# The first norm's weight row broadcast by TensorE into PSUM, its loads and the first weight loads issued together, one square pass per token tile

## The chip, the cores and the metric

One NeuronCore of a Trainium2 chip runs the whole program. The metric is device time in microseconds of one execution, the median of three runs. Five engines work beside each other: TensorE (PE) multiplies, VectorE (DVE), ScalarE (ACT) and GpSimd (POOL) do elementwise work, and SyncE (SP) issues most of the DMA transfers. Each takes its own instructions strictly in the order in which the program was scheduled, and waits where an operand is not ready.

## The reference: one hybrid decoder layer

The layer has 512 tokens of width 1024. Three residual blocks follow one another, each with an RMS norm before and after it: a token mixer (sparse attention, pooling and a spatial gating unit, all fed by one projection `w_in`), cross-attention into 256 memory tokens, and a gated MLP with a causal convolution. Everything is float32. The change touches only the very start:

```python
def rms_norm(x, g):
    xf = x.astype(F32)
    y = xf * lax.rsqrt(jnp.mean(xf * xf, axis=-1, keepdims=True) + EPS)
    return (y * g.astype(F32)).astype(x.dtype)
...
        h = rms_norm(x, mix_norm_pre[l])
        proj = h @ w_in[l]
        q, kc, vc, ksl, vsl, kw, vw, gt, pin, u, v = jnp.split(proj, IN_SPLITS, axis=-1)
```

## The kernel before

**The numbers.** A float32 matmul is made of three: both operands are split into a rounded high part and a low remainder (`split`: ACT casts the high part, another engine subtracts for the low part), and `mm3` (lines 167 to 169) adds high x high, high x low and low x high in PSUM. So each 1024-column piece of weights passes through a raw tile (`wr`), a cast into `wh` and a subtraction into `wl` before TensorE may use it, and each normed activation goes into `hTh` and `hTl`.

**The first norm.** Tokens are cut into four tiles of 128 rows (`xt[0]` to `xt[3]`). For each, `norm_T` squares the row on ACT in two halves of 512 columns (L108, the sums go through `ss` into `nt` on DVE), takes the power -0.5 on POOL (L100, `nr`), multiplies by that scale and the norm's weight row on DVE (L119, `hn`), transposes 128x128 blocks on TensorE (L122, into `tp`, two PSUM buffers), and splits the result into `hTh` (ACT, L67) and `hTl` (DVE, L68). The tile `hn` has two buffers, so a third `hn` waits for the transposes of the first. The weight row `grow` (1x1024) is needed on all 128 partitions: L252 lets POOL copy it there into `gpre`.

**The first projections.** `w_c` holds the 256 columns of `w_in` for the compressed branch, `w_k` those for the keys. `chan_halves` runs four jobs (two 128-column blocks of each) first over tokens 0 to 255 (half 0: tiles 0 and 1), then over tokens 256 to 511: 2 x 4 x 8 x 3 = 192 matmuls of 256 columns. Then come the fp32 matmuls of the compression (L367), the query projection of group 0 (`w_q`), and the value projection (columns 280 wide, four quarter loads of `w_in` through `wr`), and then attention.

**What sets the order.** The tile scheduler arranges each engine's instructions by a timeline of its own; after that each engine is in order. SP issues the loads in one row, so a load that has to wait for a buffer holds back the loads behind it. Raw weight tiles `wr` have three buffers. The pool `xp` (the start's tiles) is freed after the first norm, and its memory is used by tiles of the next stages, whose first writer waits for the old tile's last reader. POOL issues its own DMAs too: `fscr` and `cb` (L303 to L309), the tables of position biases that go through DRAM.

Of the kernel before, what the change touches and what calls it, by code (L numbers as in the profile page):

```python
# [49 lines left out]
def trunk_kernel(ctx, tc, x, mem, rel_bias, mix_norm_pre, mix_norm_post, w_in, cmp_pos, cmp_w1,  # L50
# [49 lines left out]
        nc.gpsimd.tensor_tensor(r, t, neghalf[:, :n], OP.pow)  # L100
        return r

    def norm_T(src, g, dst, i, junk, hn, pstile):
        t = None
        for half in range(2):
            ss = small("ss")[:, 0:1]
            c = slice(half * 512, half * 512 + 512)
            nc.scalar.activation(junk, src[:, c], AF.Square, accum_out=ss)  # L108
            t2 = small("nt")[:, 0:1]
            if half == 0:  # L110
                nc.vector.tensor_scalar(t2, ss, 1.0 / D, EPS, OP.mult, OP.add)
            else:
                nc.vector.scalar_tensor_tensor(t2, ss, 1.0 / D, t, OP.mult, OP.add)
            t = t2
        r = power(t, 1)
        for half in range(2):
            h = hn(half)
            c = slice(half * 512, half * 512 + 512)
            nc.vector.scalar_tensor_tensor(h, src[:, c], r, g[:, c], OP.mult, OP.mult)  # L119
            pt = pstile()  # L120
            for k in range(4):
                tr = nc.tensor.transpose(pt[:, k, :], h[:, k * P:(k + 1) * P], ident)  # L122
            o = (slice(None), i // 2, slice(half * 4, half * 4 + 4), slice(i % 2 * P, i % 2 * P + P))
            done = split(dst[0][o], dst[1][o], pt)
        return (tr,) + done
# [19 lines left out]
            if done is not None:  # L145
                done(c)

    def wload(parts, nk, ncol, pool=None, engs=(None, None)):
        pool = pool or wpool
        hi = pool.tile([P, 2048], F32R, name="wh")  # L150
        lo = pool.tile([P, 2048], F32R, name="wl")
        n = nk // 2 * ncol
        for half in range(2):
            raw = wpool.tile([P, 1024], F32, name="wr", bufs=3)
            rv = raw[:, :n].rearrange("p (k c) -> p k c", k=nk // 2)
            c0 = 0
            for src in parts:
                w = src.shape[1]
                sr = src.rearrange("(k p) c -> p k c", p=P)
                nc.sync.dma_start(rv[:, :, c0:c0 + w], sr[:, half * nk // 2:(half + 1) * nk // 2, :])  # L160
                c0 += w
            split(hi[:, half * n:half * n + n], lo[:, half * n:half * n + n], raw[:, :n], engs[half])
        return (hi[:, :2 * n].rearrange("p (k c) -> p k c", k=nk),
                lo[:, :2 * n].rearrange("p (k c) -> p k c", k=nk))
# [52 lines left out]
    with ExitStack() as at:  # L217
# [26 lines left out]
        with ExitStack() as p0:  # L244
            xp = pool_of(p0, "xp")
            xt = [xp.tile([P, D], F32, name=f"xt{i}") for i in range(TT)]
            grow = xp.tile([1, D], F32, name="grow")
            gpre = xp.tile([P, D], F32, name="gpre")
            nc.sync.dma_start(xt[0], x[0:P, :])
            nc.sync.dma_start(grow, mix_norm_pre)  # L250
            nc.sync.dma_start(xt[1], x[P:2 * P, :])
            nc.gpsimd.partition_broadcast(gpre, grow)  # L252
            idi = xp.tile([P, P], mybir.dt.int32, name="idi")
            nc.gpsimd.iota(idi, pattern=[[1, P]], base=0, channel_multiplier=-1)
            nc.vector.tensor_scalar(ident, idi, 0.0, None, op0=OP.is_equal)
            junk = xp.tile([P, 512], BF16, name="junk")

            def norm0(i):
                norm_T(xt[i], gpre, hT, i, junk,
                       lambda k: xp.tile([P, 512], F32, name="hn", tag="hn", bufs=2), tp_tile)  # L260

            norm0(0)
            norm0(1)
            w_c = wload([w_in[:, 512:768]], KT, 256, engs=(nc.gpsimd, nc.gpsimd))
            for i in range(2, TT):
                nc.sync.dma_start(xt[i], x[i * P:(i + 1) * P, :])
            w_k = wload([w_in[:, 768:896], w_in[:, 1024:1152]], KT, 256,
                        engs=(nc.gpsimd, (nc.vector, nc.gpsimd)))
            for i in range(2, TT):
                norm0(i)  # L270

            smA = xp.tile([P, P], F32, name="smA")
            smB = xp.tile([89, P], F32, name="smB")
# [675 lines left out]
```

## Time and profile before

| what | us |
|---|---|
| median of 3 runs | 801.93 |
| lowest and highest run | 801.47, 803.82 |
| profiled execution, first to last instruction | 802.6 |
| TensorE busy in it | 757.6 (94%) |
| VectorE, ScalarE, GpSimd busy | 452.7, 352.9, 128.1 |

The profiled execution gives its span only; no time around the span is shown. The span lies 0.7 us above the median and inside the spread of the three runs. "Busy" is the time an engine spends in instructions; for TensorE the ends of matmuls are modelled, so that 94% says that it seldom waits, and nothing about its peak.

### The profile page before, as it was taken

The page shows a single profiled execution, that of the slowest core. Times are in us where ns is not written, and L with a number is a line of the kernel's source. Part 1 is how long each engine was busy: PE and PEld are TensorE (multiplying, and loading weights), DVE is VectorE, ACT ScalarE, POOL GpSimd, SP SyncE. Part 2 cuts the span into 40 slices and gives each one's busy share as a digit, 9 for nine tenths or more (in the row PEclk, how much of TensorE's full clock was granted, in tenths as well). Part 3 has the DMA queues.
Part 4 walks back from the last instruction along what each step waited for, and adds up shares of the span by engine and source line. Part 5 has one row for each costly group of instructions (what it writes and reads, how often), then busy time and mean ns, then how long its engine had stood idle before and what let it go on. Part 6 is the DMA issues. An engine that isn't in the chain of part 4 may idle for free.

```text
span 802.6 us, 10783 instructions
## 1 busy us (share of the span) xinstructions
PE 757.6 (94%) x4164; PEld 655.8 (82%) x4164; DVE 452.7 (56%) x796; ACT 352.9 (44%) x645; POOL 128.1 (16%) x144
## 2 busy tenths in 40 slices
PE   0699999998999999999999999999999999999996
PEld 0598988876998889988888988888888888888884
DVE  0864557899666584328366475665655665213214
ACT  2334558667655463336354443444343344113111
POOL 1633246476510110040002000000000000000001
PEclk9999999999999999999999999999999999999998
DMA  5455314401048136320150123333233333124212
GB/s 197 109 132 142 115 30 131 158 23 31 3 147 318 58 114 202 106 77 30 53 183 28 53 79 106 105 105 94 80 90 105 105 105 105 56 76 146 75 42 105
DMA packets 65163, 80.64 MB, mean 100 GB/s; under 512 B 4079, under 2 KB 48071, under 8 KB 65112
## 3 DMA queue, kind: packets, MB, share of 16 engines
q1 hardware_dynamic: 64791, 79.77, 31.6%
q8 instruction: 33, 0.54, 0.3%
q0 software_dynamic: 320, 0.18, 0.1%
q14 instruction: 19, 0.15, 0.1%
HBM read 77.79 MB, written 2.14 MB: 100 GB/s over the span
## 4 chain that ended last, share of the span: by engine, by line
PE 84%; DVE 7%; issue 4%; ACT 3%; DMA 2%; POOL 0%; DVEq 0%; SPq 0%; ACTq 0%; POOLq 0%
PE mb L168 21%; PE mb L169 20%; PE mb L167 20%; PE mm L167 4%; PE mm L168 4%; PE mm L169 4%; PE tp L530 2%; DMA wr<-in_w_up_dram 1%; ACT wh L67 1%; DVE hn L119 1%; PE av L542 1%; PE mm L367 1%; PE av L540 1%; PE tb L122 1%; PE qk L503 1%
## 5 line engine op out<-in xcount | busy, mean ns | idle before, releaser
L68 DVE TENSOR_TENSOR wl<-wr,wh 128x1024 fp32r<-128x1024 f32 (+1 forms) x106 | 128.9, 1249 | 157.5 <-ACT wh L67 157.4
L67 ACT CAST wh<-wr 128x1024 fp32r<-128x1024 f32 (+2 forms) x125 | 122.7, 1024 | 153.6 <-PE mb L169 65.5
L169 PE MATMUL mb<-bacth,wl 128*128 128x512 f32 (+1 forms) x400 | 144.9, 363 | 0.0
L168 PE MATMUL mb<-bactl,wh 128*128 128x512 f32 (+1 forms) x400 | 144.8, 363 | 0.0
L167 PE MATMUL mb<-bacth,wh 128*128 128x512 f32 (+1 forms) x400 | 144.7, 363 | 0.0
L169 PEld LDWEIGHTS mb<-bacth,wl 128*128 128x128 f32 x400 | 75.1, 188 | 11.9
L167 PEld LDWEIGHTS mb<-bacth,wh 128*128 128x128 f32 x400 | 75.1, 188 | 12.0
L168 PEld LDWEIGHTS mb<-bactl,wh 128*128 128x128 f32 x400 | 75.2, 188 | 11.7
L100 POOL TENSOR_TENSOR nr<-n,neghalf 128x1 f32<-128x1 f32 x12 | 7.7, 643 | 466.8 <-DVE n L140 466.8
L168 PE MATMUL mb<-wl,gTh 128*128 128x512 f32 x176 | 68.5, 389 | 0.0
L169 PE MATMUL mb<-wh,gTl 128*128 128x512 f32 x176 | 68.5, 389 | 0.0
L167 PE MATMUL mb<-wh,gTh 128*128 128x512 f32 x176 | 67.5, 389 | 0.0
L68 POOL TENSOR_TENSOR wl<-wr,wh 128x1024 fp32r<-128x1024 f32 (+1 forms) x20 | 44.2, 2226 | 68.7 <-ACT wh L67 68.2
L853 ACT ACTIVATE cv<-mb,tabA,tabB 128x512 f32<-128x512 f32 x44 | 34.1, 778 | 36.6 <-PE mb L169 34.7
L854 DVE SCALAR_TENSOR_TENSOR cv<-mb,tabB,cv 128x511 f32<-128x511 f32 x44 | 32.8, 746 | 30.1 <-ACT cv L853 30.1
L518 POOL TENSOR_SCALAR pb<-pb,asm,gates 128x128 f32<-128x128 f32 (+3 forms) x64 | 43.1, 688 | 34.7 <-DVE asm L514 29.5
L509 ACT ACTIVATE pb<-pb,anm 128x128 f32<-128x128 f32 (+3 forms) x64 | 35.5, 557 | 7.7 <-DVE anm L507 7.3
L169 PEld LDWEIGHTS mb<-wh,gTl 128*128 128x128 f32 x176 | 33.0, 188 | 6.9
L168 PEld LDWEIGHTS mb<-wl,gTh 128*128 128x128 f32 x176 | 33.0, 188 | 6.9
L167 PEld LDWEIGHTS mb<-wh,gTh 128*128 128x128 f32 x176 | 33.0, 188 | 6.7
L507 DVE CUSTOM_DVE_ANT_0 pb<-qk,mbias 128x128 f32<-128x128 f32 (+3 forms) x64 | 28.7, 480 | 9.3 <-PE tp L530 6.0
L67 ACT CAST pth<-tp 128x512 fp32r<-128x512 f32 x40 | 23.1, 583 | 23.9 <-PE tp L530 21.7
(266 smaller groups left out, 1657.6 us busy)
## 6 DMA issues: line engine op xcount, KB each, us to landing
wr<-in_w_up_dram SPq DMA_DIRECT2D x44, 512.0 KB
wr<-in_w_down_dram SPq DMA_DIRECT2D x20, 512.0 KB
wr<-in_w_in_dram SPq DMA_DIRECT2D x12, 512.0 KB
wr<-in_w_mk_dram SPq DMA_DIRECT2D x8, 512.0 KB
wr<-in_w_out_dram SPq DMA_DIRECT2D x8, 512.0 KB
wr<-in_w_mv_dram SPq DMA_DIRECT2D x8, 512.0 KB
wr<-in_w_mq_dram SPq DMA_DIRECT2D x8, 512.0 KB
wr<-in_w_mo_dram SPq DMA_DIRECT2D x8, 512.0 KB
```

What stands on the lines that cost most here:

```text
L67: return (nc.scalar.copy(hi, src) if hi_eng is None else hi_eng.tensor_copy(hi, src), lo_eng.tensor_tensor(lo, src, f(hi), OP.subtract))
L68: lo_eng.tensor_tensor(lo, src, f(hi), OP.subtract))
L119: nc.vector.scalar_tensor_tensor(h, src[:, c], r, g[:, c], OP.mult, OP.mult)
L167: nc.tensor.matmul(o, lh, rh, start=first, stop=False)
L168: nc.tensor.matmul(o, lh, rl, start=False, stop=False)
L169: nc.tensor.matmul(o, ll, rh, start=False, stop=last)
L507: nc.vector.tensor_tensor_reduce(pb[:, br, :n], ob[br], mb, 1.0, BIG, OP.add, OP.min, accum_out=nm[:, h_, br:br + 1])
L509: nc.scalar.activation(pb[:, br, :n], pb[:, br, :n], AF.Exp, bias=nm[:, h_, br:br + 1], scale=-1.0, accum_out=sm[:, h_, br:br + 1])
L518: nc.gpsimd.tensor_scalar(pr[h_][:, br, :n], pr[h_][:, br, :n], sm[:, h_, br:br + 1], GV[:, i, hh, 1 + br:2 + br], OP.mult, OP.mult)
L530: tr = nc.tensor.transpose(pt[:, br * 2 + h_, :], pr[h_][:, br, j * P:(j + 1) * P], ident)
L853: nc.scalar.activation(c, o, AF.Identity, bias=tabA[:, 40 + a:41 + a], scale=tabB[:, 44 + a:45 + a])
L854: nc.vector.scalar_tensor_tensor(c[:, 1:], o[:, :S - 1], tabB[:, a:a + 1], c[:, 1:], OP.mult, OP.add)
```

## The change

The broadcast on POOL goes. Instead TensorE multiplies a row of ones (1x128) with the two halves of `grow` into two PSUM tiles, one of the tag `qk` and the one of the tag `av`, and `hn` reads its weights from there. The load of `grow` moves from SP to ACT's queue. All four token tiles and the four raw halves of `w_c` and `w_k` get memory of their own in `xp` and are issued by SP at once, in the order of the diff; before, the second half of `w_k` went through a `wr` buffer that first had to come free. Squares are taken over 1024 columns in one pass. For `w_k`'s second half the low part moves from DVE to POOL and the cast from POOL to ACT.

```diff
--- before.py
+++ after.py
@@ -100,11 +100,12 @@
         nc.gpsimd.tensor_tensor(r, t, neghalf[:, :n], OP.pow)
         return r
 
-    def norm_T(src, g, dst, i, junk, hn, pstile):
+    def norm_T(src, g, dst, i, junk, hn, pstile, parts=2):
         t = None
-        for half in range(2):
+        for half in range(parts):
             ss = small("ss")[:, 0:1]
-            c = slice(half * 512, half * 512 + 512)
+            n = D // parts
+            c = slice(half * n, half * n + n)
             nc.scalar.activation(junk, src[:, c], AF.Square, accum_out=ss)
             t2 = small("nt")[:, 0:1]
             if half == 0:
@@ -116,7 +117,8 @@
         for half in range(2):
             h = hn(half)
             c = slice(half * 512, half * 512 + 512)
-            nc.vector.scalar_tensor_tensor(h, src[:, c], r, g[:, c], OP.mult, OP.mult)
+            gc = g[half] if isinstance(g, list) else g[:, c]
+            nc.vector.scalar_tensor_tensor(h, src[:, c], r, gc, OP.mult, OP.mult)
             pt = pstile()
             for k in range(4):
                 tr = nc.tensor.transpose(pt[:, k, :], h[:, k * P:(k + 1) * P], ident)
@@ -145,20 +147,25 @@
             if done is not None:
                 done(c)
 
-    def wload(parts, nk, ncol, pool=None, engs=(None, None)):
+    def raw_load(raw, parts, nk, half):
+        ncol = sum(src.shape[1] for src in parts)
+        rv = raw[:, :nk // 2 * ncol].rearrange("p (k c) -> p k c", k=nk // 2)
+        c0 = 0
+        for src in parts:
+            w = src.shape[1]
+            sr = src.rearrange("(k p) c -> p k c", p=P)
+            nc.sync.dma_start(rv[:, :, c0:c0 + w], sr[:, half * nk // 2:(half + 1) * nk // 2, :])
+            c0 += w
+
+    def wload(parts, nk, ncol, pool=None, engs=(None, None), raws=None):
         pool = pool or wpool
         hi = pool.tile([P, 2048], F32R, name="wh")
         lo = pool.tile([P, 2048], F32R, name="wl")
         n = nk // 2 * ncol
         for half in range(2):
-            raw = wpool.tile([P, 1024], F32, name="wr", bufs=3)
-            rv = raw[:, :n].rearrange("p (k c) -> p k c", k=nk // 2)
-            c0 = 0
-            for src in parts:
-                w = src.shape[1]
-                sr = src.rearrange("(k p) c -> p k c", p=P)
-                nc.sync.dma_start(rv[:, :, c0:c0 + w], sr[:, half * nk // 2:(half + 1) * nk // 2, :])
-                c0 += w
+            raw = raws[half] if raws else wpool.tile([P, 1024], F32, name="wr", bufs=3)
+            if not raws:
+                raw_load(raw, parts, nk, half)
             split(hi[:, half * n:half * n + n], lo[:, half * n:half * n + n], raw[:, :n], engs[half])
         return (hi[:, :2 * n].rearrange("p (k c) -> p k c", k=nk),
                 lo[:, :2 * n].rearrange("p (k c) -> p k c", k=nk))
@@ -245,29 +252,39 @@
             xp = pool_of(p0, "xp")
             xt = [xp.tile([P, D], F32, name=f"xt{i}") for i in range(TT)]
             grow = xp.tile([1, D], F32, name="grow")
-            gpre = xp.tile([P, D], F32, name="gpre")
-            nc.sync.dma_start(xt[0], x[0:P, :])
-            nc.sync.dma_start(grow, mix_norm_pre)
-            nc.sync.dma_start(xt[1], x[P:2 * P, :])
-            nc.gpsimd.partition_broadcast(gpre, grow)
+            ones = xp.tile([1, P], F32, name="ones")
+            nc.vector.memset(ones, 1.0)
+            nc.scalar.dma_start(grow, mix_norm_pre)
+            raws = [[xp.tile([P, D], F32, name=f"raw{a}{b}") for b in range(2)] for a in range(2)]
+            c_parts = [w_in[:, 512:768]]
+            k_parts = [w_in[:, 768:896], w_in[:, 1024:1152]]
+            for i in range(2):
+                nc.sync.dma_start(xt[i], x[i * P:(i + 1) * P, :])
+            for half in range(2):
+                raw_load(raws[0][half], c_parts, KT, half)
+            for i in range(2, TT):
+                nc.sync.dma_start(xt[i], x[i * P:(i + 1) * P, :])
+            for half in range(2):
+                raw_load(raws[1][half], k_parts, KT, half)
             idi = xp.tile([P, P], mybir.dt.int32, name="idi")
             nc.gpsimd.iota(idi, pattern=[[1, P]], base=0, channel_multiplier=-1)
             nc.vector.tensor_scalar(ident, idi, 0.0, None, op0=OP.is_equal)
-            junk = xp.tile([P, 512], BF16, name="junk")
+            junk = xp.tile([P, D], BF16, name="junk")
+            gpre = [qk_tile(), ps.tile([P, S], F32, name="av", tag="av", bufs=1)]
+            for half in range(2):
+                nc.tensor.matmul(gpre[half], ones, grow[:, half * 512:half * 512 + 512], start=True, stop=True)
 
             def norm0(i):
                 norm_T(xt[i], gpre, hT, i, junk,
-                       lambda k: xp.tile([P, 512], F32, name="hn", tag="hn", bufs=2), tp_tile)
+                       lambda k: xp.tile([P, 512], F32, name="hn", tag="hn", bufs=2), tp_tile, 1)
 
             norm0(0)
             norm0(1)
-            w_c = wload([w_in[:, 512:768]], KT, 256, engs=(nc.gpsimd, nc.gpsimd))
-            for i in range(2, TT):
-                nc.sync.dma_start(xt[i], x[i * P:(i + 1) * P, :])
-            w_k = wload([w_in[:, 768:896], w_in[:, 1024:1152]], KT, 256,
-                        engs=(nc.gpsimd, (nc.vector, nc.gpsimd)))
+            pl = (nc.gpsimd, nc.gpsimd)
+            w_c = wload(c_parts, KT, 256, engs=pl, raws=raws[0])
             for i in range(2, TT):
                 norm0(i)
+            w_k = wload(k_parts, KT, 256, engs=pl, raws=raws[1])
 
             smA = xp.tile([P, P], F32, name="smA")
             smB = xp.tile([89, P], F32, name="smB")
```

Three places show how instructions move. The first is the beginning of the program on POOL, before. `ISA` ahead of another row of the same line is an instruction that the compiler puts there by itself.

```order
L254 ISA
L254 IOTA idi 128x128
L635 MEMSET pw 128x256
L641 MEMSET sa 128x16
L641 MEMSET sb 128x16
L252 ISA
L252 ISA gpre<-grow 128x1024
L100 ISA
L100 TENSOR_TENSOR nr<-nt,neghalf 128x1 x2
L68 TENSOR_TENSOR wl<-wr,wh 128x1024 x2
L100 TENSOR_TENSOR nr<-nt,neghalf 128x1 x2
```

The same place on POOL in the change.

```order
L270 ISA
L270 IOTA idi 128x128
L100 TENSOR_TENSOR nr<-nt,neghalf 128x1 x2
L68 TENSOR_TENSOR wl<-raw_112,wh 128x1024
L68 TENSOR_TENSOR wl<-raw_113,wh 128x1024
L100 TENSOR_TENSOR nr<-nt,neghalf 128x1 x2
L68 TENSOR_TENSOR wl<-raw_114,wh 128x1024
L68 TENSOR_TENSOR wl<-raw_115,wh 128x1024
L598 AFFINE_SELECT mixs_75<-mixs_75 128x512
L320 DMA fscr<-fs 8x640
```

The broadcast and the two `ISA` rows of L252 and L100 are gone; the powers follow the iota directly. The low parts of the weights now number four ahead of the DMAs, two between the powers of tiles 0, 1 and those of tiles 2, 3.

The second place is the beginning on ACT, before (`xt_104` to `xt_107` are the four token tiles).

```order
L108 ACT_TABLE_LOAD
L108 ACTIVATE junk,ss<-xt_104 128x512 x2
L108 ACTIVATE junk,ss<-xt_105 128x512 x2
L67 CAST wh<-wr 128x1024
L67 CAST hTh<-tp 128x4x128
L67 CAST wh<-wr 128x1024
L67 CAST hTh<-tp 128x4x128
L108 ACTIVATE junk,ss<-xt_106 128x512 x2
L67 CAST hTh<-tp 128x4x128
L108 ACTIVATE junk,ss<-xt_107 128x512
L67 CAST hTh<-tp 128x4x128
L108 ACTIVATE junk,ss<-xt_107 128x512
```

The same place on ACT in the change (`raw_112`, `raw_113` are the halves of `w_c`, `raw_114`, `raw_115` those of `w_k`).

```order
L257 DMA grow<-in_mix_norm_pre_dram 1x1024
L109 ACT_TABLE_LOAD
L109 ACTIVATE junk,ss<-xt_104 128x1024
L109 ACTIVATE junk,ss<-xt_105 128x1024
L67 CAST wh<-raw_112 128x1024
L67 CAST wh<-raw_113 128x1024
L67 CAST hTh<-tp 128x4x128 x2
L109 ACTIVATE junk,ss<-xt_106 128x1024
L109 ACTIVATE junk,ss<-xt_107 128x1024
L67 CAST hTh<-tp 128x4x128
L67 CAST wh<-raw_114 128x1024
L67 CAST hTh<-tp 128x4x128
```

Both casts of `w_c` now stand ahead of the first `hTh`, and the squares of tiles 2 and 3 ahead of the third `hTh`, the first one of tile 1.

The third place is on SP, before: the loads from the one-hot table to the last quarter of the raw value weights that stands near them (`wr` of 128x2x128 and 128x2x152 are quarters of the value projection, `sgg` and `sgb` the rows of the gating unit's norm).

```order
L285 DMA oh<-in_onehot_dram 64x640
L160 DMA wr<-in_w_in_dram 128x4x128 x2
L286 DMA pc<-in_pconst_dram 128x34
L290 DMA rb<-in_rel_bias_dram 32x8
L579 DMA sgg<-in_sgu_norm_g_dram 128x256
L160 DMA wr<-in_w_in_dram 128x4x256
L579 DMA sgb<-in_sgu_norm_b_dram 128x256
L580 DMA mixs_75<-in_sgu_w_dram 128x4x128
L638 DMA pw<-in_pool_w_dram 64x64 x4
L160 DMA wr<-in_w_in_dram 128x4x256
L160 DMA wr<-in_w_in_dram 128x2x128
L160 DMA wr<-in_w_in_dram 128x2x152
```

The same stretch of SP in the change, from the four compression loads to the value weights.

```order
L380 DMA w_10_549<-in_cmp_w_dram 128x8x128
L380 DMA w_11_551<-in_cmp_w_dram 128x8x128
L404 DMA w2k<-in_cmp_w_dram 128x64 x2
L406 DMA w2v<-in_cmp_w_dram 128x64
L409 DMA b2v<-in_cmp_b_dram 128x64
L596 DMA sgg<-in_sgu_norm_g_dram 128x256
L596 DMA sgb<-in_sgu_norm_b_dram 128x256
L157 DMA wr<-in_w_in_dram 128x2x128
L157 DMA wr<-in_w_in_dram 128x2x152
L655 DMA pw<-in_pool_w_dram 64x64 x4
L157 DMA wr<-in_w_in_dram 128x2x128
L157 DMA wr<-in_w_in_dram 128x2x152
```

`sgg` and `sgb` stood ahead of all value loads; now they stand behind the compression loads and ahead of three of the four quarters. They also take memory that POOL's bias-table DMAs read, so that they wait for those DMAs. From the value projection on, all five engines have the same order in both kernels.

## Rows read from the trace of the kernel before

**Rows 1.** The page: span, and TensorE's busy time, share and instructions.
```profile
span 802.6 us, 10783 instructions
...
PE 757.6 (94%) x4164; PEld 655.8 (82%) x4164; DVE 452.7 (56%) x796; ACT 352.9 (44%) x645; POOL 128.1 (16%) x144
```

**Rows 2.** Waits of TensorE, whole span, then 31 to 120 us (total, times, longest).
```profile
PE tp L122 <- DVE hn L119: 22.5, 1, 22.5
...
PE mm L405 <- ACT hv L381: 0.4, 1, 0.4
```

**Rows 3.** Timeline of POOL, 0 to 60 us: start, duration, instruction [idle before].
```profile
1.16 0.23 POOL L254 IOTA idi<- 128x128 int32 x1 [0.66 <-POOLq L930]
...
11.88 1.30 POOL L252 PARTITION_BROADCAST gpre<-grow  x1 [10.13 <-issue]
21.08 0.59 POOL L100 TENSOR_TENSOR nr<-nt,neghalf 128x1 f32<-128x1 f32 x1 [7.89 <-issue]
...
24.05 5.10 POOL L68 TENSOR_TENSOR wl<-wr,wh 128x1024 fp32r<-128x1024 f32 x2
...
54.09 4.78 POOL L309 DMA_DIRECT2D cb<-fscr  x8 [2.61 <-DMA fscr<-fs]
```

**Rows 4.** The chain that ended last, in order of time: the row's load.
```profile
1.24 2.88 DMA grow<-in_mix_norm_pre_dram
```

**Rows 5.** Timeline of ACT, 0 to 45 us.
```profile
4.55 0.63 ACT L108 ACTIVATE junk<-xt 128x512 bf16<-128x512 f32 x1 [2.48 <-DMA xt<-in_x_dram]
...
6.06 0.63 ACT L108 ACTIVATE junk<-xt 128x512 bf16<-128x512 f32 x1
...
8.52 1.04 ACT L67 CAST wh<-wr 128x1024 fp32r<-128x1024 f32 x1 [0.99 <-DMA wr<-in_w_in_dram]
...
36.15 1.07 ACT L67 CAST hTh<-tp 128x512 fp32r<-128x512 f32 x2 [2.44 <-PE tp L122]
```

**Rows 6.** Timeline of DVE, 24 to 37 us.
```profile
24.12 2.83 DVE L119 SCALAR_TENSOR_TENSOR hn<-xt,nr,gpre 128x512 f32<-128x512 f32 x1 [0.67 <-POOL nr L100]
26.87 0.68 DVE L68 TENSOR_TENSOR hTl<-tp,hTh 128x512 fp32r<-128x512 f32 x1
...
34.23 2.35 DVE L292 TENSOR_SCALAR rbn<-rb 32x32 f32<-32x32 f32 x1
```

**Rows 7.** Waits of SP's own queue, 0 to 16 us.
```profile
SPq L280 <- DMA xt<-in_x_dram: 1.1, 1, 1.1
SPq L279 <- DMA xt<-in_x_dram: 1.0, 1, 1.0
...
SPq L278 <- DMA wr<-in_w_in_dram: 0.2, 1, 0.2
```

**Rows 8.** Timeline of SP's queue, 10 to 31 us.
```profile
10.31 0.25 SPq L278 DMA_DIRECT2D smA<-in_sgu_b_dram  x1
11.60 0.29 SPq L279 DMA_DIRECT2D smA<-in_conv_b_dram  x1
12.96 0.29 SPq L280 DMA_DIRECT2D smA<-in_conv_w_dram  x1
...
30.62 2.43 SPq L638 DMA_DIRECT2D pw<-in_pool_w_dram  x4
```

**Rows 9.** Timeline of TensorE's matmuls, 30 to 79 us.
```profile
30.45 1.08 PE L122 MATMUL tp<-ident,hn 128*128 128x128 f32 x4 [1.67 <-DVE nt L111]
31.18 0.78 PE L167 MATMUL mm<-hTh,wh 128*128 128x256 f32 x2
...
32.40 0.41 PE L168 MATMUL mm<-hTl,wh 128*128 128x256 f32 x1
32.61 0.41 PE L169 MATMUL mm<-hTh,wl 128*128 128x256 f32 x1
...
47.42 1.04 PE L301 MATMUL tp<-oh,rbn 64*32 64x512 f32 x2
...
78.34 0.29 PE L167 MATMUL mm<-wh,hTh 128*128 128x280 f32 x1
```

## The prediction

> **What bounds the kernel now.** I read the page first: a span of 802.6 us in which TensorE is busy for 757.6 us [rows 1]. So 45 us are left in which it does nothing, and the waits of TensorE say that half of them are one wait: 22.5 us for the first `hn`, before TensorE has done anything at all [rows 2]. From 31 to 120 us it waits for another engine only 0.4 us [rows 2]. That is the picture of a kernel that starts late and then runs on a full TensorE: whatever lets TensorE start earlier is gained at the end, as long as the work behind the start is fed at the same pace.
>
> Why the start is late stands in the timeline of POOL. The iota runs at 1.16. Then nothing for 10.1 us, put down to "issue", until the broadcast at 11.88, which takes 1.3 us; then 7.9 us of "issue" again until the first power at 21.08 [rows 3]. The weight row itself had landed by 4.12 [rows 4], and ACT began the squares at 4.55 [rows 5], so neither data nor squares were late. In the order, these two gaps are where the `ISA` rows of L252 and L100 stand; I read them as POOL loading other code for the broadcast and then loading the old code again.
>
> **The change part by part.** *The broadcast goes.* With it go both `ISA` rows, so I take 10.1 + 1.3 + 7.9 us off POOL's path and let the first power run as soon as its sum is there. The Trainium skill (GPSIMD Engine Reference, section Instruction dispatch) says that the first call into freshly loaded code pays about 6 us that no row shows; two such loads would make 12 us where the trace has 18. It leaves open whether the power would pay once in any case, which would speak against the change; that is the first rival below.
>
> *When the norm is ready now.* Tile 0 is squared from 4.55 on. A pass of 1024 columns isn't in the trace; from above it costs the 1.51 us between the starts of two tiles' passes, from below the 1.04 us of a cast of that size [rows 5]. I take 1.2, with its read-back, nearer to the cast, because one start and one read-back of two fall away. Sum by 5.8, `nt` 0.2, power 0.6 [rows 3], `hn` 0.7 (as an elementwise pass of that size with one operand in PSUM, 0.68 [rows 6]), four transposes 1.1 [rows 9]: `tp` is full at about 8.9.
>
> *The row by TensorE.* The load of the row takes 2.9 us [rows 4] from about 0.8, so 3.7. A float32 product of 512 columns runs in two passes, 1.04 us at the pace of 47 us [rows 9]. At the start the pace is half: 256 columns every 0.21 us at 32.4, which is the 1.2 GHz level [rows 9]; so 2.1 us each, ready at 5.8 and 7.9. The first `hn` is needed from 6.6, its second half from 7.3. At worst 0.6 us late, and the next paragraph hides it.
>
> *What sets the new start.* ACT's order decides. Ahead of the first `hTh` stand both casts of `w_c`, and the second one needs the second raw half. SP's waits give its landing: a load goes only when the one eight places ahead has landed, and L278, L279 and L280 waited so for that half, for tile 2 and for tile 3 [rows 7], at 10.31, 11.60 and 12.96 [rows 8]. These loads keep their places in SP's row, so I keep these times. Then on ACT: cast 1.04 to 11.35, two `hTh` 1.07 to 12.4 [rows 5], the squares of tiles 2 and 3 at 1.2 each to 14.8 (both tiles have landed), and the first `hTh` of tile 1 to **15.4**. Only then can the matmuls of half 0 begin, since each reads tiles 0 and 1. By the bounds of the square pass it is 15.1 to 16.0. Everything else is there: the transposes of tile 1 need a free `tp` (`hTl` 0.7 after 11.9) and end at 13.7 and 14.8; POOL's first two low parts, 2.55 each [rows 3], run from 9.55 to 14.6. `gpre` and the first norm have 2.4 us to spare against the cast at 11.35.
>
> *The sum.* The first matmul was at 31.18 [rows 9], now at 15.4: 15.8 us. I take off 0.3 for the first low part of tile 1, which ends 0.7 after its high part while two matmuls of 0.2 run ahead, and 0.3 for the second, which stands on DVE behind the two `hn` of tile 2 and ends at 18.1, just when TensorE arrives. Left: **15.2 us**.
>
> *Is the feed behind it fast enough?* The low parts of `w_k` end on POOL at 18.9 and 21.4; TensorE wants them after 48 matmuls and 8 transposes, 24 of them at 0.21 and the rest at half that, so near 24. The load of `rb` now goes right behind the one-hot table, near 17.5, and lands by 20.4 if it takes as long as the row's load. Its DVE row stands ahead of tile 3's `hn`; before, it took 2.35 us beside a low part on POOL [rows 6], so I let it end with POOL's at 21.4. Tile 3's first transposes stand at about 24.4 on TensorE and need `hn` at 22.1: 1.5 to 2 us to spare. The low part of `w_k` that leaves DVE costs nothing there. The value loads: in the change they wait on SP behind `sgg` and `sgb`, which wait for POOL's `cb` transfers. Those were issued from 54.09 to 58.87 [rows 3]; moved by 15.2 they end at 43.7 and land by 46.6. Two loads of 0.5, the pool weights' 2.4 [rows 8], three quarters at 0.8, a landing of 2.9, a cast and a low part of 2 make 57.3. The value matmuls began at 78.34 [rows 9], so they want this at 63.1: 6 us to spare. From there on all engines have one order in both kernels, and the rest moves as a block.
>
> The span becomes 802.6 - 15.2 = 787.4. The profiled execution lies 0.7 above the median of the runs, so the median would be **786.7**.
>
> **The rivals.** *The power pays for its first call anyway.* Then the gap of 7.8 us stands between the first sum at 6.0 and the power: power at 13.8, `hn` to 15.1, transposes to 16.2, two `hTh` to 17.4, squares to 19.8, start at 20.4, and 791.7. Against it: there is no `ISA` row ahead of the power any more, and the first low part on POOL, another kind of operation, ran at 24.05 with no gap [rows 3]. The skill's first-call cost of the page above is this case.
>
> *The feed breaks behind the start.* DVE stands at `rb`, and each microsecond that this load lands after about 22 keeps tile 3's transposes, and with them all matmuls of `w_k` behind them, waiting. The same happens if `hn` is locked out while POOL runs: beside the low parts one `hn` took 2.83 us [rows 6]. Against that, `hTl` beside it, with one operand in PSUM, took 0.68 [rows 6], and `hn` now has its weights in PSUM too. Locked out until 18.9, tile 2's second `hn` would cost 2 us. Together 1 to 5 us: 788 to 792.
>
> *Slower.* SP is the place: `sgg` waits for the `cb` transfers with three quarters of the value weights behind it. If these transfers stayed where they are on the clock, landing at 61.8, the last low part would be ready at 72.5 instead of 57.3, TensorE would stand still for 9.4 us, and 5.8 us would be left: 796.1. To come out slower by 2.4 us, the least that a measurement here can tell from no change (0.3%), `sgg` would have to go after 70, 8 us later than it could before. I see nothing that puts it there. No change at all would need it to go near 67.6.
>
> **How the numbers follow.** Forecast 0.76 (785.5 to 788.5 by the bounds of the square pass and half a microsecond either way), first-call cost 0.08, feed 0.12, no change 0.02, slower 0.02. The first three are all faster by over 0.3%, so faster 0.95 (a little off for what I have not seen), same 0.03, slower 0.02. The range reaches up through the feed case to 792, and down to 784 for loads that land earlier than in the trace of before.
>
> **What would show it.** Right: on POOL the first power near 6 with no idle time put down to "issue" ahead of it; the two products of the row before 8; the first matmul of the projection at 15 to 16, released by ACT's `hTh` of tile 1; no wait of TensorE over 1 us from there to 105 us; the value matmuls near 63. Wrong: a power after 10; a wait of TensorE for `hn` of tile 3 or for DVE's `rbn`; a wait ahead of the value matmuls; or a gain at the start that shrinks later although the order is the same.

## The result, and the profile after

| what | before | after |
|---|---|---|
| median, us (4 runs each) | 801.70 | 789.28 |
| lowest and highest | 800.83, 803.82 | 788.38, 791.53 |
| profiled execution, span | 802.6 | 789.6 |
| TensorE busy in it | 757.6 (94%) | 766.1 (97%) |

The ratio is 0.9844, with a 95% interval of 0.9824 to 0.9864: faster by 1.6%, or 12.4 us. The forecast was 786.7. The profiled execution after is the one of 791.53, the slowest of its four runs; the spans of the four are 786.4, 787.0, 787.9 and 789.6.

The page of after, span and busy times:

```profile
span 789.6 us, 10781 instructions
...
PE 766.1 (97%) x4168; PEld 661.2 (84%) x4168; DVE 445.8 (56%) x792; ACT 353.0 (45%) x638; POOL 125.6 (16%) x143
```

TensorE is busy 8.5 us longer than before [rows 1]. The two products of the row make 4 us of that; for the rest the same work must have run more slowly somewhere, and the timeline of TensorE will show where. First POOL, the timeline of after (start, duration, instruction, idle time before):

```profile
0.91 0.23 POOL L270 IOTA idi<- 128x128 int32 x1 [0.40 <-POOLq L947]
6.05 0.56 POOL L100 TENSOR_TENSOR nr<-nt,neghalf 128x1 f32<-128x1 f32 x1 [4.90 <-DVE nt L112]
...
8.52 4.67 POOL L68 TENSOR_TENSOR wl<-raw,wh 128x1024 fp32r<-128x1024 f32 x2 [0.43 <-ACT wh L67]
...
37.09 4.77 POOL L326 DMA_DIRECT2D cb<-fscr  x8 [1.61 <-DMA fscr<-fs]
```

The first power stands at 6.05, and what it waited for is `nt`, its operand. The two stretches of "issue" [rows 3] are gone. ACT, the timeline of after:

```profile
4.62 1.06 ACT L109 ACTIVATE junk<-xt 128x1024 bf16<-128x1024 f32 x1 [2.01 <-DMA xt<-in_x_dram]
...
8.86 1.05 ACT L67 CAST wh<-raw 128x1024 fp32r<-128x1024 f32 x1 [0.42 <-DMA raw<-in_w_in_dram]
9.81 1.07 ACT L67 CAST hTh<-tp 128x512 fp32r<-128x512 f32 x2
10.77 1.07 ACT L109 ACTIVATE junk<-xt 128x1024 bf16<-128x1024 f32 x1
...
11.96 1.06 ACT L109 ACTIVATE junk<-xt 128x1024 bf16<-128x1024 f32 x1
...
13.01 0.57 ACT L67 CAST hTh<-tp 128x512 fp32r<-128x512 f32 x1
```

This is the order of the prediction, cast, two `hTh`, two squares, `hTh` of tile 1, and the cast that begins it waits for the second raw half. That half is there at 8.86; the prediction had 10.31. TensorE, the timeline of after:

```profile
2.30 2.04 PE L275 MATMUL qk<-grow,ones 1*128 1x512 f32 x2 [2.30 <-DVE rbn L310]
...
13.63 0.80 PE L174 MATMUL mm<-hTh,wh 128*128 128x256 f32 x2 [0.43 <-ACT hTh L67]
...
18.58 0.41 PE L174 MATMUL mm<-hTh,wh 128*128 128x256 f32 x1
18.80 0.41 PE L175 MATMUL mm<-hTl,wh 128*128 128x256 f32 x1
...
20.04 0.28 PE L176 MATMUL mm<-hTh,wl 128*128 128x256 f32 x1
20.16 0.28 PE L174 MATMUL mm<-hTh,wh 128*128 128x256 f32 x1
...
50.92 1.09 PE L422 MATMUL mm<-w2v,hv 128*128 128x64 f32 x4 [0.94 <-ACT hv L398]
...
52.49 0.63 PE L175 MATMUL mm<-hTl,wh 128*128 128x512 f32 x1
52.92 0.63 PE L176 MATMUL mm<-hTh,wl 128*128 128x512 f32 x1
...
66.25 0.29 PE L174 MATMUL mm<-wh,hTh 128*128 128x280 f32 x1
...
781.66 0.39 PE L176 MATMUL mb<-wh,gTl 128*128 128x512 f32 x1
```

The first projection product stands at 13.63, 17.55 us earlier than before [rows 9]. Products of 256 columns follow at 0.21 us, the 1.2 GHz level, until 19; before, this pace lasted from 31.2 to 33.4 only. Near 51 TensorE waits 0.94 us for `hv`, and behind that 512 columns take 0.43 us, again the 1.2 GHz level, until 57. The windows view shows this second stretch in the granted clock (columns: window, length, busy time and count of PE, PEld, DVE, ACT and POOL, clock, DMA share, GB/s):

```profile
50.00:60.00 10.00, 9.08 (x28) 7.35 (x29) 3.87 (x10) 2.60 (x8) 3.98 (x3) 0.66 0.55 160
...
170.00:180.00 10.00, 8.90 (x44) 7.89 (x45) 8.68 (x26) 6.94 (x20) 5.54 (x7) 0.66 0.14 48
...
410.00:420.00 10.00, 8.22 (x44) 6.63 (x43) 8.32 (x17) 4.27 (x10) 1.73 (x3) 1.00 0.17 53
```

The same view of the kernel before, at the places of the program that answer to the last two:

```profile
180.00:190.00 10.00, 7.46 (x42) 6.41 (x43) 9.78 (x29) 7.50 (x22) 6.37 (x10) 0.83 0.26 86
...
420.00:430.00 10.00, 8.13 (x43) 6.54 (x42) 8.01 (x18) 4.95 (x13) 2.54 (x4) 0.97 0.26 83
430.00:440.00 10.00, 10.00 (x69) 9.30 (x67) 6.16 (x14) 3.66 (x11) 2.05 (x4) 0.86 0.01 2
```

Between 160 and 200 the clock falls in both; at 420 to 440 it fell before, and not after. The view doesn't show the first stretch: it reads 1.00 from 10 to 20 as well, so that the level there is read from the pace of the products alone. Followed from one matmul to its partner in the other trace, the lead over the profiled execution before goes like this (the repeats are the first and the eleventh experiment below, the same kernel with spans of 786.6 and 786.9):

| place (us in before) | forecast | after | repeat | second repeat |
|---|---|---|---|---|
| first projection product (31.18) | 15.8 | 17.55 | 16.90 | 16.64 |
| first compression product (57.91) | 15.2 | 15.41 | 15.00 | 14.87 |
| first product that reads `hv` (65.81) | 15.2 | 14.89 | 14.47 | 14.36 |
| first value product (78.34) | 15.2 | 12.09 | 14.47 | 14.35 |
| first `w_out` product (241.01) | 15.2 | 11.20 | 14.10 | 14.08 |
| last matmul (794.56) | 15.2 | 12.90 | 15.91 | 15.55 |

What sets the profiled execution of after apart from the repeats is 2.8 us between the third row and the fourth and 0.5 to 0.6 us between the fourth and the fifth, both where its clock was lower. The last row gains 1.5 to 1.8 us in all three, by the fall that the profiled execution before had at 420. Waits of TensorE after, whole span:

```profile
PE tp L547 <- DVE pcl L68: 2.4, 1, 2.4
PE qk L275 <- DVE rbn L310: 2.3, 1, 2.3
PE tp L124 <- DVE hTl L68: 1.8, 1, 1.8
...
PE mm L422 <- ACT hv L398: 0.9, 1, 0.9
```

The wait of 22.5 us [rows 2] is gone, and nothing of its size has come in its place; L547's was there before, with 2.4 us as well. The second line is the wait of the row's first product; that `rbn` released it is only the profile's inference, and in the second repeat the same product waits 3.4 us for the load of `grow`.

### The profile page after: what moved, and what is told of

It reads as the page before. It is cut to its first block, busy times and chain, and to the rows that moved or that the text cites. A ratio compares the mean times of both kernels' runs of the same rounds, so it can differ in the third digit from the quotient of the medians.

```text
span 789.6 us, 10781 instructions
## 1 busy us (share of the span) xinstructions
PE 766.1 (97%) x4168; PEld 661.2 (84%) x4168; DVE 445.8 (56%) x792; ACT 353.0 (45%) x638; POOL 125.6 (16%) x143
## 4 chain that ended last, share of the span: by engine, by line
PE 85%; DVE 6%; ACT 3%; issue 2%; SPq 1%; DMA 1%; POOL 0%; DVEq 0%; ACTq 0%; POOLq 0%
PE mb L175 21%; PE mb L176 21%; PE mb L174 21%; PE mm L174 4%; PE mm L175 4%; PE mm L176 4%; PE tp L547 2%; DMA wr<-in_w_up_dram 1%; ACT wh L67 1%; PE av L559 1%; PE mm L384 1%; PE av L557 1%; PE tb L124 1%; PE qk L520 1%; PE qk L519 1%
## 5 line engine op out<-in xcount | busy, mean ns | idle before, releaser
L67 ACT CAST wh<-wr 128x1024 fp32r<-128x1024 f32 (+2 forms) x122 | 119.6, 1024 | 151.7 <-PE mb L176 65.5
L100 POOL TENSOR_TENSOR nr<-n,neghalf 128x1 f32<-128x1 f32 x12 | 7.4, 620 | 465.4 <-DVE n L142 465.4
L68 POOL TENSOR_TENSOR wl<-wr,wh 128x1024 fp32r<-128x1024 f32 (+1 forms) x17 | 36.6, 2169 | 70.0 <-ACT wh L67 70.0
L67 ACT CAST pth<-tp 128x512 fp32r<-128x512 f32 x40 | 23.1, 583 | 24.7 <-PE tp L547 22.5
```

The costliest lines, as they stand in the source:

```text
L67: return (nc.scalar.copy(hi, src) if hi_eng is None else hi_eng.tensor_copy(hi, src), lo_eng.tensor_tensor(lo, src, f(hi), OP.subtract))
L68: lo_eng.tensor_tensor(lo, src, f(hi), OP.subtract))
```

## The experiments

Each ran beside the kernel before on the same chip (medians 801.75 to 802.49). The theory is that of the prediction: the two stretches of "issue" around POOL's broadcast made the start late. "Lead" is meant as in the table above.

**1. The changed kernel again.** No edit.

> The changed kernel once more, beside the kernel before, for the spread and the clock of more runs. My theory: TensorE starts 15 to 17.5 us earlier and everything behind moves as a block; what the profiled run gained less (13.0 us of span) it lost where TensorE ran at 1.2 GHz (13.6 to 19.7 us, and 51 to 57 us). Then the spans of the runs follow their mean granted clock, and at equal clock the two kernels differ by 15 to 16 us of span. Rival: part of the gain is given back by waits, the same in every run; then the difference at equal clock is 12 to 13 us.

789.30 us, ratio 0.9841 (0.9819 to 0.9863). A third time, as the eleventh experiment, beside the last two fill kernels:

> The changed kernel once more, on the chip and in the rounds of the two fill kernels. Every theory: 788.5 to 790.

788.84 us, ratio 0.9833 (0.9811 to 0.9855). The spans of these 13 runs of the changed kernel go from 786.0 to 790.6, median 787.0. The windows view of the first repeat, where the wait for `hv` was just as long:

```profile
50.00:60.00 10.00, 8.96 (x42) 7.20 (x42) 5.30 (x13) 4.25 (x11) 4.41 (x3) 1.00 0.53 160
```

So the same wait is followed by the low clock in one execution and not in another.

The theory of the first repeat was that at equal mean clock the two kernels differ by 15 to 16 us of span, its rival 12 to 13. Neither fits. The 55 listed runs of the kernel before that stood beside the experiments have a median span of 800.5, which is 13.5 above 787.0, and runs of the two kernels with the same mean granted clock (0.993 to 0.996) lie on average 13.3 to 14.5 us apart.

**2. The row by TensorE alone.** The kernel before with this edit; loads, buffers and squares stay.

```diff
-            nc.gpsimd.partition_broadcast(gpre, grow)
+            gpre = [qk_tile(), ps.tile([P, S], F32, name="av", tag="av", bufs=1)]
+            for half in range(2):
+                nc.tensor.matmul(gpre[half], ones, grow[:, half * 512:half * 512 + 512], start=True, stop=True)
```

> The kernel before with one part of the change alone: the weight row broadcast by TensorE into PSUM. The order of the loads, the raw buffers and the two square passes are as before. My theory (POOL's two code loads kept the first norm waiting): first power near 6 us, first matmul of the projection at 15 to 17 us, time 787 to 791. Rival (the loads issued at once bring the gain): first matmul after 25 us and a time over 797.

798.69 us, ratio 0.9946 (0.9926 to 0.9965): far above what I expected. The start is there, the first projection product 15.3 us earlier than before; at the first value product the lead is 2.95. Waits of TensorE, waits and timeline of SP's queue, and the timeline of TensorE:

```profile
PE mm L371 <- DMA w<-in_cmp_w_dram: 2.3, 1, 2.3
```

```profile
SPq L367 <- PE tp L305: 11.9, 1, 11.9
```

```profile
38.58 7.70 SPq L367 DMA_DIRECT2D w<-in_cmp_w_dram  x4
```

```profile
15.90 0.80 PE L168 MATMUL mm<-hTh,wh 128*128 128x256 f32 x2 [0.33 <-ACT hTh L67]
...
44.61 1.89 PE L371 MATMUL mm<-bk,w 128*128 128x62 f32 x16
48.76 10.17 PE L371 MATMUL mm<-bk,w 128*128 128x62 f32 x48 [2.25 <-DMA w<-in_cmp_w_dram]
```

SP holds the compression weights (`w`) back for 11.9 us, until the product that reads the one-hot table has been made: their tiles take memory of the start's pool. They are issued at 38.6; TensorE runs 16 products in 1.89 us, waits 2.25 us, and makes the other 48 at half that pace. In the kernel before the same hold-up cost nothing, because TensorE itself was late.

**3. The loads without TensorE's row.** The changed kernel with POOL's broadcast put back (the diff of experiment 2 the other way round).

> The changed kernel with that one part undone: POOL broadcasts the row into SBUF again, all else as changed. My theory: the two gaps of 10 and 8 us on POOL are back, first power near 21 us, first matmul at 26 to 29 us, time 797 to 801. Rival (the loads bring the gain): 788 to 791.

802.27 us, ratio 0.9998 (0.9987 to 1.001). Timeline of POOL:

```profile
9.51 1.30 POOL L272 PARTITION_BROADCAST gpre<-grow  x1 [8.12 <-issue]
18.52 0.59 POOL L100 TENSOR_TENSOR nr<-nt,neghalf 128x1 f32<-128x1 f32 x1 [7.71 <-issue]
```

Alone, the loads and squares bring nothing: the two stretches of "issue" stand there again. The first projection product comes at 28.37, 2.8 us earlier than before, and of that 1.0 us is left at the last matmul.

**12. A broadcast that nobody reads.** The changed kernel plus one broadcast of 16 columns. POOL has three rows more; every other row of every engine stands as in the changed kernel.

```diff
+            spare = xp.tile([P, 16], F32, name="spare")
+            nc.gpsimd.partition_broadcast(spare, grow[:, 0:16])
```

> The changed kernel, with one broadcast on POOL of 16 columns whose result nobody reads; it stands on POOL behind the iota, and every other row of every engine stands as in the changed kernel. Theory (POOL's path to the first power was two stretches of about 8 to 10 and 7.8 us around the broadcast, whatever it carries): the first power at 17 to 20 instead of 6, the first projection product at 25 to 27, and 10 to 12 us of the gain gone: median 799 to 802. Rival: the stretches belong to the wait for the whole row and its 1024 columns, and a small broadcast that nobody waits for costs 1 to 2 us: median 789 to 792.

800.49 us, ratio 0.9978 (0.9964 to 0.9993). Timeline of POOL:

```profile
10.02 0.29 POOL L289 PARTITION_BROADCAST spare<-grow  x1 [8.63 <-issue]
18.29 0.59 POOL L100 TENSOR_TENSOR nr<-nt,neghalf 128x1 f32<-128x1 f32 x1 [7.98 <-issue]
```

As the theory had it, the first power comes at 18.29, and the first projection product at 25.06. The broadcast itself takes 0.29 us and costs 11 us of time. So the price is neither the row's 1024 columns nor a wait for them, but the two stretches around the instruction, 8.6 and 8.0 us.

**8. The row, and other memory.** Experiment 2 plus one unused tile of 16 KB per partition in the start's pool. It takes as much memory as the four raw tiles of the change, so that the next stage's tiles lie elsewhere and the scheduler puts their loads earlier; the raw weights still go through `wr`.

```diff
+            pad = xp.tile([P, 4 * D], F32, name="pad")
+            nc.vector.memset(pad[:, 0:1], 0.0)
```

> The kernel before with the row by TensorE alone, plus one unused tile of 16 KB per partition in the pool of the start, so that the tiles of the next stage lie on other memory; loads, wr buffers and squares stay as before. Theory: what the own raw tiles of the change bring is mostly this: the compression weights (w1) no longer wait on SP for the one-hot product (11.9 us, loads at 38.6) but go at 22 to 28, TensorE does not wait 2.3 us for them, and the stretch of 15 us at the 1.2 GHz level behind that wait goes: median 788 to 792. Rival: it is the early loads of w_k themselves, and the memory changes nothing: 796 to 800.

791.47 us, ratio 0.9872 (0.9853 to 0.989). SP's timeline and TensorE's:

```profile
25.01 4.04 SPq L369 DMA_DIRECT2D w<-in_cmp_w_dram  x4
```

```profile
42.73 7.25 PE L373 MATMUL mm<-bk,w 128*128 128x62 f32 x64
```

The weights go 13.6 us earlier and the 64 products run in one piece. In ratios, 0.0074 of the 0.0102 between experiment 2 and the changed kernel are there, 5.9 of 8.2 us. The pad changes where the tiles lie and, with that, SP's order; the trace doesn't part these two. What brings the other 2.2 us was not tested by itself. The profile of this kernel has a wait of 2.0 us for `vt` at 53 us, which the changed kernel doesn't have, but it is the slowest of its four runs.

**7. Squares in two passes again.** The changed kernel, with `parts` of 2.

```diff
-                       lambda k: xp.tile([P, 512], F32, name="hn", tag="hn", bufs=2), tp_tile, 1)
+                       lambda k: xp.tile([P, 512], F32, name="hn", tag="hn", bufs=2), tp_tile, 2)
```

> The changed kernel with the squares in two passes of 512 columns again. Theory (ACT's order sets the start): the passes of tiles 0 and 1 lie ahead of the landing of the first raw half and cost little, those of tiles 2 and 3 stand on the path: 2 x 0.3 us, so the first projection product 0.6 to 1.0 later and the median 0.3 to 1.0 above the changed kernel's. Rival: the pass is hidden by loads or by the slow pace behind the start: less than 0.3 us of difference at the compression.

790.16 us, ratio 0.9852 (0.9837 to 0.9867). My theory missed: from the cast that waits for the second raw half to the first projection product it is 4.67 us (9.82 to 14.49), against 4.77 (8.86 to 13.63) with one pass, and the lead at the compression is 15.08, the repeat's 15.00. The scheduler put the second half of tile 3's square behind the first `hTh` of tile 1. The one pass brings nothing that these runs show.

**4, 5, 9. Work for TensorE in the gaps of the start.** The stretch at the 1.2 GHz level behind the start is 6 us long, so filler products whose result nobody reads were put behind the row's products and between the transposes of tiles 0 and 1. The three kernels differ in the PSUM tiles that these take: one tile of `mm` (4), two of `mm` (5), two of `tp` ahead of two of `mm` (9). The core of 9, `g1` being the last product so far and `f1` the last transpose of tile 0 or filler behind it:

```diff
+            for fill in (tp_tile(), tp_tile()):
+                with after(g1):
+                    g1 = nc.tensor.matmul(fill[:, 0, :], ones, grow[:, 0:128], start=True, stop=True)
...
+            for fill in (mm_tile(), mm_tile()):
+                with after(f1):
+                    f1 = nc.tensor.matmul(fill[:, :224], ident, xt[0][:, 0:224], start=True, stop=True)
```

> The changed kernel with two idle products added on TensorE (256 columns behind the broadcast, 448 columns between the transposes of tiles 0 and 1), whose results nobody reads. My theory: the stretch at 0.21 us per 256 columns after 13.6 us is so long (6 us, where the kernel before had 2) because TensorE had done little before it; with the products it ends by 17.5 us and 1 to 2 us are gained. Rival: the products do nothing for the clock; the stretch ends at 19 to 20 us as before and the time is the same within 0.5 us.

> The changed kernel with the two filler products of the fill kernel, but each in a PSUM tile of its own, so that the program takes two tiles of the tag mm more and not one. Theory: the filler did what it should (projection at the pace of 0.115 us from 13.64 on, lead over the kernel before 18.0 us at the compression), and the fill kernel lost it again because one more tile swapped the two mm buffers for the rest of that pool's life, so that a tile of the next pool (mb) lay on a buffer that was still read: a wait of 5.3 us at 229 and about 2 us at the 1.2 GHz level behind it. Then that wait is gone here, no wait of TensorE over 3 us stands after 20 us, the span is near 786, and the median 786.5 to 789. Rival: extra work on TensorE at the start costs later whatever tiles it uses: the wait stays and the median is 797 to 801.

> The changed kernel with filler products at the start again, now so that the tags take PSUM in the changed kernel's order (tp ahead of mm, an even number of tiles of each). Theory: the first two fill kernels lost their gain because the first filler tile gave mm the banks that tp has in the changed kernel, so that a tile of the next pool (mb) came to lie on a bank that a late subtraction still read; the order of waits on TensorE says this wait is not there now. Then the pace is 0.115 from the first projection product on, the lead at the compression is 16 to 18 us, no wait over 3 us stands after 20 us, and the median is 786 to 788, 1 to 3 below the changed kernel. Rival: what the filler gains at the start is lost behind it by falls of the clock: 788.5 to 790.

Measured: 799.84 us (ratio 0.997, 0.9958 to 0.9982), 796.03 (0.9924, 0.9911 to 0.9936) and 789.74 (0.9846, 0.9823 to 0.9869). In 4 the pace is 0.115 us almost from the first product on, and the lead at the compression 18.0. Timeline of TensorE in 4:

```profile
14.59 0.28 PE L176 MATMUL mm<-hTh,wl 128*128 128x256 f32 x1
14.70 0.28 PE L174 MATMUL mm<-hTh,wh 128*128 128x256 f32 x1
```

Then, at 230 us, waits of TensorE in 4 and in 5:

```profile
PE mb L174 <- DVE km L68: 5.3, 1, 5.3
```

```profile
PE mb L174 <- DVE km L68: 2.6, 1, 2.6
```

Kernel 9, where the tags come upon PSUM in the changed kernel's order, has no such wait. So my theory of 5, an odd number of tiles, was at most half of it: the order of first use counts as well. That it does so by giving the tags their banks is argued only; no trace here shows addresses. But 9 doesn't gain either. Its lead is 17.9 at the compression and 14.9 at the first value product, with these waits of TensorE on the way,

```profile
PE mm L174 <- DVE vt L432: 1.2, 1, 1.2
PE mm L430 <- ACT hv L406: 0.9, 1, 0.9
```

and a granted clock of 0.83 from 50 to 60. The rival of 9 held: what is gained at the start is lost behind it, by the clock and, which the rival did not name, by the wait of 1.2 us. Nor does the filler always speed the start up: in 5, and in 10, which has the start of 9 word for word, the slow pace was there in spite of it, and the lead at the compression 15.9 and 15.5.

**6 and 10. The wait for `hv`.** In 6 the two products that read `hv` are written behind the query projection; 10 is kernel 9 with two products of 192 columns in that wait.

```diff
+            q_proj(0, w_q)
             for g in range(2):
                 po = mm_tile()[:, :64]
                 nc.tensor.matmul(po, hid[1 + g].rearrange("p h c -> p (h c)"), w2v, start=True, stop=True)
...
-            q_proj(0, w_q)
```

> The changed kernel with the two small value products of the compression (L422, which wait 0.9 us for hv) written behind the query projection instead of ahead of it; up to there all engines have the same order. Theory: that wait is what lets TensorE's clock fall in some executions (6 us at the 1.2 GHz level behind it in the profiled one, 2.4 us lost); without it 0.9 us are gained in every execution and the fall goes: median 786.5 to 788.5, PEclk 1.00 from 50 to 60. Rival: the fall comes from the 62-column products ahead of it, and would come just so without the wait: 0 to 0.9 us, median 788.4 to 789.8.

> As the third fill kernel, and two more products of 192 columns in the wait for hv at 50 us. Theory: the fall of the clock at 50 to 57 us in some executions needs that wait; with the wait filled PEclk is 1.00 from 50 to 60 in every profile, and the median lies 0.5 to 2 below the third fill kernel, 785 to 787.5. Rival: the fall comes with or without it: no difference over 0.5 us to the third fill kernel.

789.84 us (ratio 0.9848, 0.9827 to 0.9869) and 790.47 us (0.9837, 0.981 to 0.9863): both theories missed, there is no gain over the changed kernel. In 6 the wait for `hv` turned into one of 0.9 us for `kc`, ahead of the value products. In 10 it is 0.2 us. The windows view of 10:

```profile
50.00:60.00 10.00, 9.68 (x44) 7.66 (x44) 4.92 (x12) 3.61 (x10) 3.91 (x3) 1.00 0.51 160
410.00:420.00 10.00, 7.47 (x33) 5.96 (x32) 7.16 (x15) 5.76 (x15) 1.10 (x2) 0.83 0.00 1
```

The low stretch at 50 is gone in both profiles, but it was gone in the two repeats of the changed kernel too, wait and all. So neither run tells whether the wait makes it. None of these kernels beats the changed one.

## Why the prediction was right, and where its number came from

**The broadcast: right, and shown.** The first power was to stand near 6, without "issue": it stands at 6.05, and the two products of the row have ended by then. Experiments 3 and 12 put the stretches back and lose 11 to 13 us with them. The first rival, a first call of 7.8 us that the power pays anyway, is out. That the stretches are POOL loading code stays a reading: the trace of experiment 12 has a pair of `MODIFY_POOL_CONFIG` rows, which the timeline leaves out, at the head of each stretch (1.37 and 10.25), but also one ahead of the iota (1.05), and that one costs nothing. The Trainium skill (GPSIMD Engine Reference, section Instruction dispatch) has the invisible price of a first call into loaded code at about 6 us. By that, as an estimate, the two loads would be 12 us; experiment 12 has 8.6 and 8.0, the kernel before 10.1 and 7.9 [rows 3], and the measured figures are the ones to use.

**The start: right in mechanism, 1.8 us off in size.** ACT's order set it, as forecast. The step that failed is "these loads keep their places in SP's row, so I keep these times". The load of `grow` had left SP's row, so each of them moved up, and the second half of `w_c` was there at 8.86 and not at 10.31 (9.50 and 9.77 in the repeats). But the landing also spreads from one execution to the next. Experiment 6, which has the changed kernel's start word for word, got it at 10.47; its timelines of ACT and TensorE:

```profile
10.47 1.05 ACT L67 CAST wh<-raw 128x1024 fp32r<-128x1024 f32 x1 [0.39 <-DMA raw<-in_w_in_dram]
```

```profile
15.25 0.80 PE L174 MATMUL mm<-hTh,wh 128*128 128x256 f32 x2 [0.43 <-ACT hTh L67]
```

So the same loads in the same order land up to 1.6 us apart, and the forecast's 10.31 and 15.4 stand at the late end of that; that the smaller row made the landing earlier is not shown. From the landing to the first product the sum had 5.1 us, and all four traces have 4.8. One sum is off without effect: by its terms the first `tp` is full at 8.4 and not at 8.9, and the cast behind it hides both.

**The pace behind the start: missed by about as much.** The sum took the whole difference at the first product as gained, less 0.6. But the slow pace lasted 6 us instead of 2.3, and by the compression the lead was 15.41, not 17.55. The prediction had the number in hand: its check of the feed counts 24 products at 0.21 us, where the kernel before made about 10 at that pace and the changed one about 24. Some 14 more at 0.1 us each are 1.4 us, an estimate from these rows, and the sum put them at nothing without a reason. That 15.41 agrees with the forecast 15.2 is luck: two errors of some 2 us cancel.

**The feed: held, with one load left out of the check.** No wait of TensorE over 1 us stands between the first projection product and 105 us. `rb` was read at 18.97 (20.4 forecast as landed), tile 3's second `hn` began at 21.42 (wanted by 22.1), and no `hn` beside a low part on POOL took over 0.75 us. The value products began without a wait. But the prediction never asked for the compression weights, and experiment 2 shows that they are what breaks: with a start 15 us earlier they come too late unless the tiles lie elsewhere. An unused tile of the size of the four raw tiles is enough for that; the prediction gave these tiles no part in the gain. About half of the change's worth stands on this: by the ratios TensorE's row alone is worth 4.3 us, with the pad 10.3, the whole change 12.5.

**Behind 50 us: "the rest moves as a block" failed in the profiled execution.** TensorE waited 0.94 us for `hv` where it had waited 0.42 [rows 2], and the clock behind it was down to the 1.2 GHz level for 6 us: 2.8 us of lead lost by the first value product. Experiments 3 and 12, whose start is late, wait 0.94 us for `hv` as well, and 2 and 8, whose start is early, 0.42 and 0.43, so the longer wait comes with the changed kernel's order and not with the earlier start. In both repeats the lead at the first value product was 14.4 to 14.5. So one of the prediction's signs of being wrong came: a gain at the start that shrinks later although the order is the same. From the value products on, each stretch without a fall of the clock did move as a block, to within 0.15 us.

**The number: the span of 787.4 came out by two errors that cancel, and the step to a time was wrong.** The median span of 13 runs is 787.0. But the sum started from an execution of 802.6, and the 55 listed spans of the kernel before have a median of 800.5. From median to median the gain is 13.5 us: the sum's start was 2.1 us too high and its gain 1.7 us too large. The prediction then subtracted 0.7, because the span of 802.6 lay 0.7 above the median *time*. But a time is longer than the span of the same run: by 1.66 to 1.82 us in all runs of the kernel before for which both are listed, and by 1.8 to 2.0 in runs of the changed kernel. 787.4 and 1.9 make 789.3, and 789.28 was measured. The one listed run of the kernel before with a span of 802.6 has a time of 804.26, 2.6 above the median of 801.70, so the profiled execution of before was a long one, and that is why a lead of 15.2 us over it became 12.4 us between the medians. Its fall of the clock near 430 is in no profile of the changed kernel and is probably part of the reason; the fall between 160 and 200 is not, since every profile here has it. The two rivals on the far side, feed and `sgg`, did not come: `sgg` went at 36.95, the value loads behind it at 41.8.

## What to carry to other kernels

A single instruction of another kind on POOL cost 11 to 13 us here, at a place where nothing but POOL's next small operation waits; look for "issue" on either side of it, and ask whether another engine can make the same few bytes. When a start moves earlier, list every load that the next stage needs with the buffer it waits for: the same product of the row was worth 4 us or 10 here, without and with a pad that moved the next tiles and their loads. And compare spans with spans and times with times, over several runs: the profiled executions lay 2.1 us (before) and 2.6 us (after) above the median span of their kernels.

## What the runs showed of the hardware that was not expected

- Two stretches of "issue" on POOL, 8.1 to 10.1 us ahead of a broadcast and 7.7 to 8.0 us behind it, independent of its size (1024 columns 1.30 us, 16 columns 0.29 us).
- TensorE's clock fell behind some waits and not behind others of the same length: at 50 us behind 0.94 us in the profiled execution (0.66 in that window), not in two repeats (1.00). Near 415 us it was 0.83 in experiment 10 and 1.00 in the repeats of the changed kernel. Places with a fall in one execution and none in another changed the lead by 1.5 to 2.8 us; the spans of the changed kernel spread over 4.6 us, the longest three (789.3 to 790.6) at the lowest mean clock, 0.988.
- The slow pace of the start is not in the granted clock of the windows view: 1.00 from 10 to 20 us, while 256 columns took 0.21 us each instead of 0.115.
- The same loads in the same order landed 1.6 us apart from one execution to the next (8.86 to 10.47 us).
- A stall is dear by what follows: in experiment 2 the wait was 2.25 us, but the 48 products behind it took 0.21 us each instead of 0.11, 5 us more.
- Which tags the filler tiles at the start came from decided over a wait 200 us later: 5.3, 2.6 or 0 us for `mb`. That PSUM banks are the reason is argued only.
